# Five of the third group's value tiles ahead of a block stage, three behind it, and all eight heads' queries as blocks

## The chip, the cores and the metric

The kernel runs on one core of one Trainium2 chip. The metric is device time in microseconds (us) of one execution: the median of 3 runs is 1455.4 us (1455.23 to 1455.44). A core has a matrix engine (PE), three others for elementwise work (VectorE or DVE, ScalarE or ACT, GpSimd or POOL), and SyncE (SP), which here only issues transfers. Each engine runs its own instructions strictly in the order in which the program lists them.

## The reference

One encoder layer in fp32 on 1024 tokens of width 1024. All branches read one input projection of the normalised input:

```
h = rms_norm(x) * norm_w
z = h @ w_in        # columns: attention q,k,v of 3 groups x 8 heads x 64, g_a (512),
                    # q_b, zf_fwd, zf_bwd, i_b, g_b (1024 each), zgate_a, zgate_b (1024 each)
# (A) for group g with (window, dilation) in (128,1), (512,4), (2048,16):
s = rms_norm(q) . rms_norm(k) / 8 + bias;  p = exp(s - max);  o_g = p v / sum(p)
o_a = the groups' o_g merged per head, weighted by denominators and maxima
y_a = (o_a * silu(g_a)) @ w_proj_a
# (B) per head of 128: f = lb + (1 - lb) * sigmoid(zf);  S_t = diag(f_t) S_(t-1) + (1 - f_t) i_t^T
o_b = rms_norm(q_b . S forward + q_b . S backward) * silu(g_b);  y_b = o_b @ w_proj_b
x + (sigmoid(zgate_a) * y_a + sigmoid(zgate_b) * y_b) @ w_out
```

Products keep fp32 accuracy: each operand is split into a high part in the matrix engine's fp32r format and the remainder (low part), and high x high, high x low and low x high are summed, three matmuls for each.

## The kernel before

All tiles are 128 partitions by 512 columns unless said otherwise. A weight page of that shape is loaded (`raw`, or `qraw` for blocks), copied by ACT to its high part `whi`, and the low part `wlo` is formed by POOL or DVE. Nine pairs `whi`/`wlo` can be held (RING).

Stages, in the order of PE:
- Values. `tok_group` makes one tile of 128 tokens by 512 value columns: 8 pages by 3 matmuls = 24, called a unit here (PE rows `gp`). A group of values is 8 units, which all read the same 8 pages; the pages come free as the last unit or pair of units goes through them. The first and second groups of heads come first, then the third (`for g in (1, 2)`), in the order of tokens 4, 5, 6, 7, 0, 1, 2, 3. Meanwhile DVE and ACT form the sums `S0` to `S3` of quarters of the input.
- Block stage (`start_quads`, `run_quads`). A block is a product of two 2 x 2 block matrices in 7 products instead of 8 ("11", T1, T2, "21", T3, "22", T4), each 4 x 3 = 12 matmuls into banks `qA`, `qE`, `qC`. Four raw pages make a block's weights (a quad); differences for the T products are formed in place in `qraw` by DVE. The ring of raw pages (QRAW long) gives slots out in order. 27 blocks: 12 for queries and keys (with norms over `nss`), 6 for output gates, 3 for queries `q_b` of heads 0 to 5 (QB), 4 and 2 for the gates.
- i and b columns of the values of branch B (`evac_early`): 16 units in two groups of 8 (`ib_pages`), then 4 units (`T_group`) for the queries of heads 6 and 7. During these `attention_start` opens the attention tiles and queues their loads: the saved quarter `h10D`, keys `ak`, queries `aq`, `abias`, values `av`. The small matmuls of attention (scores `sc`, transposes `pT`, outputs `o`) are put between the units' matmuls by `burst`. DVE adds bias and takes the maximum (`as`, `mst`), ACT takes exponentials.
- Merge of the groups, then branch B head by head, then the output projections.

What sets the order: a planner (`Plan`, `Builder`) runs while the program is written. It keeps a clock for each engine, and at each `tick` puts out the waiting tasks whose inputs it expects to be ready; `b.until` lets its PE clock run on until a condition holds. The instructions then stand in that order for good. `b.BACK` says how far an engine's planned clock may be ahead of PE's for a task still to be put on it.

All engine calls pass through one helper, so every row of the profile names line 58.

Of the kernel before, what the change touches and what calls it, by code (L numbers as in the profile page):

```python
# [26 lines left out]
LEAD = 4  # L27
TAIL, LATE = 4, 4
EARLY = 8
QB = 6  # L30
QRAW, SPARE = 6, 7
LOWS = ("T2", "T4")
SQ, EA = 2, 6
VR, PT = 10, 8
# [2 lines left out]
def _dram(ap, offset, dims):  # L37
    return bass.AP(tensor=ap.tensor, offset=ap.offset + offset, ap=dims)
# [491 lines left out]
class Ring:  # L530
# [30 lines left out]
    def soon(self, n=1):  # L561
        return self.room(n) and self.when(n) <= self.b.p.t["pe"] + self.b.AHEAD
# [60 lines left out]
def hybrid_block(ctx, tc, a, out):  # L623
    b = Builder(ctx, tc, a)
    a_, v_, g_, t_, s_ = b.p.act, b.p.dve, b.p.pool, b.p.pe, b.p.sp
# [7 lines left out]
    last = {}  # L633

    def psum(n):
        order = lambda which: sorted(which, key=lambda i: b.p.free(last[i][0]) if i in last else 0.0)
        b.gps = Banks(b, psp, last, order(range(n)))
        b.bank = Banks(b, psp, last, order(range(n, 8)))
# [11 lines left out]
    stage = b.ring(stg, "stage", 3, [128, 512])  # L650

    def store(dst, t):

        def f():
            s_.dma_start(dst, t)
            stage.done(t)
        b.task("sp", [t], f, 1)
# [4 lines left out]
    some = lambda p, n: [wi[p + k] for k in range(n)]  # L662
# [7 lines left out]
    for k in range(6):  # L670
        blocks += qk[2 * k:2 * k + 2] + sg[k:k + 1] + ([("qb", 2 * k - 2)] if 0 < k <= QB // 2 else [])
    blocks += [("gb", k) for k in range(4)] + [("ga", 0), ("ga", 2)]

    def block_pages(kind, *at):
        if kind == "sg":
            return (*gate_pages(*at), *gate_pages(at[0], at[1] + 1))
        if kind == "ga":
            return tuple(some(72 + 2 * at[0], 4))
        if kind == "qb":
            return (*q_pages(at[0]), *q_pages(at[0] + 1))  # L680
        if kind == "gb":
            return tuple(_dram(wi, (100 + 20 * at[0] + 4 * k) * 65536 + 256 + 128 * col, [[512, 128], [65536, 4], [1, 128]])
                         for col in range(2) for k in range(2))
        g, hv, e = at
        p = 24 * g + 8 + 8 * hv
        return tuple(_dram(wi, (p + 4 * k) * 65536 + 128 * (2 * e + col), [[512, 128], [65536, 4], [1, 128]])
                     for col in range(2) for k in range(2))

    items = some(0, 8) + some(24, 8) + some(48, 8)
    items += [block_pages(*x) for x in blocks]  # L690
    for k in range(2):
        items += ib_pages(k)
    for h in range(QB, EARLY):
        items += q_pages(h)
# [34 lines left out]
    def hs(e, d, t0, n):  # L729

        return hq[e][t0 // 512, d // 4][:, d % 4, t0 % 512:t0 % 512 + n]
# [123 lines left out]
    vD = dr.tile([3, S, 512], F32, name="vD")  # L855
# [28 lines left out]
    def tok_group(p0, t0, evac, last=False, first=None):  # L884
        def step(d):
            wh, wl = b.w[p0 + d]
            vh, vl = first(d) if first else (hs(0, d, t0, 128), hs(1, d, t0, 128))
            return [(vh, wh), (vh, wl), (vl, wh)]

        gr = dict(k=8, step=step, evac=evac, need=lambda d: p0 + d + 1)  # L890
        if last:
            gr["free"] = lambda d: p0 + d + 1
        return gr
# [18 lines left out]
    pos = 0  # L912

    put = {}

    def evac_v(g, t0, scale=None, ring=None):
        def f(ps):
            t = stage.get()  # L920
            a_.activation(t, ps, AF.Copy, **({"scale": scale()} if scale else {}))
            (ring or b.gps).done(ps)
            put[g] = put.get(g, 0) + 1
            if t0 < 0:
                def both():
                    s_.dma_start(vD[g, S - 64:S], t[0:64])
                    s_.dma_start(vD[g, 0:64], t[64:128])
                    stage.done(t)
                b.task("sp", [t], both, 1)
            else:  # L930
                store(vD[g, t0:t0 + 128], t)
        return f

    for d in range(LEAD):
# [96 lines left out]
    def u_group(k, j, t0):  # L1031
        c = slice(128 * j, 128 * j + 128)
        return tok_group(pos, 0, evac_v(1, t0, scale=lambda: rs[k][:, j:j + 1], ring=None if k == 0 else b.bank), first=lambda d: [x[:, c] for x in u_of(k, d)])

    grs = [dict(u_group(1, 3, -64), ring=b.bank)] + [u_group(0, j, A0 + 128 * j) for j in range(4)]
# [70 lines left out]

    for g in (1, 2):
        if g == 2:
            grs = [tok_group(pos, 128 * i, evac_v(g, 128 * i), last=(k >= 6))
                   for k, i in enumerate((4, 5, 6, 7, 0, 1, 2, 3))]  # L1110
        for k, gr in enumerate(grs[:6]):
            if g == 1 and k < 5:
                continue
            b.run_unit([gr])
            if g == 2 and k >= 3:
                blocks_start()
        b.run_unit(grs[6:])
        pos += 8
    b.until(lambda: blocks_start() or "p" in blk)

# [78 lines left out]
         for op, tk in {"11": (0, 0), "21": (0, 1), "T4": (1, 1)}.items()}  # L1199
    for op, k in {"T1": 0, "T2": 1, "T3": 2, "22": 3}.items():  # L1200
        A[op] = [[x[:, c] for c in range(4)] for x in blk["S"][k]]
    b.BACK = 1.2
    b.run_quads(A, [{"qk": put_qk, "sg": put_sg, "ga": put_ga, "gb": put_gb, "qb": put_qb}[x[0]](*x[1:]) for x in blocks],
                [blk["spare"] if x[0] == "qk" else stage for x in blocks])
    b.BACK = 2.5
# [3 lines left out]
    att = {}  # L1209

    def attention_start(now=False):
        if att or not (now or (not b.small and b.quiet())):
            return
        b.drain()
        gctx.close()
        sctx.close()
        p = hctx.enter_context(tc.tile_pool(name="h10b", bufs=1, side="right"))
        psum(2)
        b.eager, b.SLACK = True, 0.25
        ap = actx.enter_context(tc.tile_pool(name="attn", bufs=1))  # L1220
        for n, k, shape in (("v", VR, [128, 256]), ("q", 2, [128, 2, S]), ("k", 2, [128, 2, S]),
                            ("s", 5, [128, 4, 256]), ("pt", PT, [128, 2, 2, 128]), ("os", 2, [128, 2, 2, 128]),
                            ("bias", 2, [128, 4, 256])):
            att[n] = b.ring(ap, "a" + n, k, shape)
        for e in range(2):
            hq[e][1, 0] = p.tile([128, 4, 512], F32R, name=f"hb{'hl'[e]}")
        for c in range(4):
            b.task("sp", [], lambda c=c: back_load(c), 1, stage.soon)
        for o, g in enumerate((1, 2, 0)):
            for hv in range(2):  # L1230
                soon = lambda n, k=2 * o + hv: att[n].soon() and (k == 0 or b.wire(3.5))
                for n, f in (("k", load_k), ("q", load_q), ("bias", load_bias)):
                    b.task("sp", [], lambda g=g, hv=hv, f=f: f(g, hv), 2, lambda n=n, soon=soon: soon(n))
                for i in ((7, 0, 1, 2, 3, 4, 5, 6) if g == 0 else range(8)):
                    b.task("sp", [], lambda g=g, hv=hv, i=i: load_v(g, hv, i), 2, lambda soon=soon: soon("v"))

    def back_load(c):
        t = stage.get()
# [22 lines left out]
    def load_v(g, hv, i):  # L1261
        t = att["v"].get()
        c = slice(256 * hv, 256 * hv + 256)
        if g == 0 and i == 0:
            s_.dma_start(t[0:64], vD[g, 0:64, c])
            s_.dma_start(t[64:128], vD[g, S - 64:S, c])
        elif g == 0:
            s_.dma_start(t, vD[g, 128 * i - 64:128 * i + 64, c])
        else:
            R = (4, 8)[g - 1]  # L1270
            r, half = divmod(i, 8 // R)
            s_.dma_start(t, vD[g].rearrange("(u r) c -> r u c", r=R)[r, 128 * half:128 * half + 128, c])
        V[g, hv, i] = t
# [294 lines left out]
    def evac_early(pr, i):  # L1568
        def f(ps):
            t = stage.get()  # L1570
            a_.activation(t, ps, AF.Copy)
            b.gps.done(ps)
            store(ibD[pr, i], t)
        return f

    def evac_qe(h, u):
# [4 lines left out]
            store(qD[h, u], t)  # L1581
        return f

    for pr in range(2):
        grs = [tok_group(pos, 128 * i, evac_early(pr, i), last=(i >= 6)) for i in range(8)]
        for k in range(7):
            if pr == 0 and k == 4:
                attention_start(True)
                b.until(lambda: att.get("h", 0) == 4)
            b.run_unit(grs[k:k + 1] if k < 6 else grs[6:])  # L1590
            attention_start()
            merge_maybe()
        pos += 8
    for h in range(QB, EARLY):
        for u in range(2):
# [642 lines left out]
    for half in range(2):  # L2238
        for j in range(8):
            def step(d, half=half, n=pos + j):  # L2240
# [4 lines left out]
            gr = dict(k=4, step=step, evac=evac_ya(j, half), need=lambda d, n=pos + j: n + 1,  # L2245
                      ready=lambda half=half: all((d, half) in OA for d in range(4)))
# [179 lines left out]
```

## Time and profile before

| | |
|---|---|
| median of 3 runs | 1455.4 us |
| the profiled execution, span | 1454.89 us, 1453.1 us |
| PE busy | 1444.3 us, 99% |
| DVE, ACT, POOL busy | 968.1, 894.9, 340.3 us |
| third group's value units, last matmul | 142.4 us |
| block stage on PE | 142.65 to 680.7 us |
| first scores of attention | 697.27 us |

Busy time on PE is a sum of overlapping matmuls; the distance from one start to the next is what a matmul adds to the time. In rows of the timeline the columns are start, duration, engine and line, operation, output<-inputs, shapes, count, and in brackets the engine's idle time before it with what ended it.

### The profile page before, as it was taken

Reading aid. Unit: us, or ns where it says so; the run is one execution under the profiler, and the core shown is the slowest. Engines: PE = TensorE matmul, PEld = TensorE weight load, DVE = VectorE, ACT = ScalarE, POOL = GpSimd, SP = SyncE. Lnnn points to the kernel's source line nnn. Section 1 sums busy time; section 2 is a strip of 40 time slices with the busy share of each in tenths; the row PEclk is TensorE's granted clock in tenths of the full one; section 3 lists DMA queues with packets and bytes.
Section 4 is the critical chain, followed back from the end, with each engine's and each line's share of the span. In section 5 each row is a group of like instructions: output and inputs, shape, how many; then the busy total and the mean of one; then the engine's idle time right before and its main releaser. Section 6 shows DMA issues by size and latency. Waiting matters only on the chain.

```text
span 1453.1 us, 22946 instructions
## 1 busy us (share of the span) xinstructions
PE 1444.3 (99%) x7930; PEld 1197.2 (82%) x7930; DVE 968.1 (67%) x1901; ACT 894.9 (62%) x1900; POOL 340.3 (23%) x356
## 2 busy tenths in 40 slices
PE   9999999999999999999999999999999999999998
PEld 8788888888888888888888778888888888788887
DVE  6673678678685788331564649487878786358973
ACT  7743767466565676443688852497777784558461
POOL 0102434464523433333002000031222221001011
PEclk9999999999999999999999999999999999999999
DMA  7746567777643334324848449354444453778665
GB/s 238 181 143 196 165 195 162 192 153 170 148 123 102 98 105 114 111 102 144 280 144 282 151 118 326 123 141 105 126 109 125 110 138 75 225 240 220 181 154 136
DMA packets 194992, 230.75 MB, mean 159 GB/s; under 512 B 46083, under 2 KB 118043, under 8 KB 194364
## 3 DMA queue, kind: packets, MB, share of 16 engines
q1 hardware_dynamic: 180188, 203.93, 45.0%
q0 software_dynamic: 13824, 25.17, 11.7%
q8 instruction: 62, 1.02, 0.3%
q14 instruction: 54, 0.44, 0.1%
q10 hardware_dynamic: 864, 0.19, 0.1%
HBM read 169.29 MB, written 81.43 MB: 173 GB/s over the span
## 4 chain that ended last, share of the span: by engine, by line
PE 90%; DVE 5%; ACT 3%; DMA 1%; issue 1%; SPq 0%; POOL 0%; ACTq 0%; DVEq 0%
PE gp L58 25%; PE qA L58 20%; PE qE L58 10%; PE sA L58 6%; PE qC L58 5%; PE sE L58 5%; PE u L58 3%; PE o L58 3%; PE oB L58 3%; PE pT L58 2%; PE sc L58 2%; PE nss L58 2%; DVE Bc L58 1%; PE U L58 1%; DVE S L58 1%
## 5 line engine op out<-in xcount | busy, mean ns | idle before, releaser
L58 POOL TENSOR_TENSOR wlo<-qraw,whi 128x512 fp32r<-128x512 f32 x135 | 194.3, 1444 | 381.8 <-ACT whi L58 293.8
L58 ACT ACTIVATE whi<-qraw 128x512 fp32r<-128x512 f32 x189 | 117.7, 626 | 100.8 <-DVE qraw L58 43.1
L58 DVE TENSOR_TENSOR qraw<-qraw,qraw 128x512 f32<-128x512 f32 x108 | 100.0, 927 | 39.0 <-POOL wlo L58 28.0
L58 PE MATMUL gp<-hh,whi 128*128 128x512 f32 x264 | 109.7, 416 | 0.0
L58 PE MATMUL gp<-hh,wlo 128*128 128x512 f32 x264 | 103.6, 393 | 0.0
L58 PE MATMUL gp<-hl,whi 128*128 128x512 f32 x264 | 103.0, 390 | 0.0
L58 ACT ACTIVATE as<-as,neg 128x192 f32<-128x192 f32 (+2 forms) x192 | 83.8, 442 | 16.8 <-DVE neg L58 16.7
L58 ACT ACTIVATE whi<-raw 128x512 fp32r<-128x512 f32 x92 | 57.6, 627 | 43.8 <-PE gp L58 18.7
L58 PE MATMUL qA<-hh,whi 128*128 128x512 f32 x216 | 84.4, 391 | 0.0
L58 PE MATMUL qA<-hh,wlo 128*128 128x512 f32 x216 | 84.3, 390 | 0.0
L58 DVE CUSTOM_DVE_ANT_0 as<-sc,abias 128x192 f32<-128x192 f32 (+2 forms) x192 | 56.0, 348 | 42.4 <-PE sc L58 27.1
L58 PE MATMUL qA<-hl,whi 128*128 128x512 f32 x216 | 84.0, 389 | 0.0
L58 POOL COPY mm<-Bc 128x8 f32<-128x8 f32 x64 | 32.2, 534 | 205.6 <-DVE Bc L58 123.6
L58 PE MATMUL gp<-whi,hh 128*128 128x512 f32 x192 | 78.6, 409 | 0.0
L58 PE MATMUL gp<-wlo,hh 128*128 128x512 f32 x192 | 75.2, 391 | 0.4 <-DVE wlo L58 0.4
L58 PE MATMUL gp<-whi,hl 128*128 128x512 f32 x192 | 75.0, 391 | 0.0
L58 DVE TENSOR_TENSOR wlo<-qraw,whi 128x512 fp32r<-128x512 f32 x54 | 37.3, 691 | 49.6 <-ACT whi L58 49.6
L58 DVE SCALAR_TENSOR_TENSOR ny<-ny,spare 128x512 f32<-128x512 f32 x48 | 67.4, 1405 | 1.6
L58 ACT ACTIVATE ny<-ny 128x512 f32<-128x512 f32 x96 | 60.8, 633 | 4.0 <-DVE ny L58 0.8
L58 PEld LDWEIGHTS gp<-hh,wlo 128*128 128x128 f32 x264 | 49.5, 188 | 11.0
L58 POOL DMA_DIRECT2D wlo<-in_w_in_dram x36 | 31.5, 875 | 113.6 <-ACT wlo L58 97.8
L58 PEld LDWEIGHTS gp<-hh,whi 128*128 128x128 f32 x264 | 49.8, 188 | 8.3
(306 smaller groups left out, 4208.2 us busy)
## 6 DMA issues: line engine op xcount, KB each, us to landing
qraw<-in_w_in_dram SPq DMA_DIRECT2D x108, 256.0 KB, 3.8
raw<-in_w_in_dram SPq DMA_DIRECT2D x84, 256.0 KB, 3.7
qkD<-ny SPq DMA_DIRECT2D x48, 256.0 KB, 2.8
wlo<-in_w_in_dram POOLq DMA_DIRECT2D x36, 256.0 KB, 4.4
sg<-sgD SPq DMA_DIRECT2D x32, 256.0 KB, 3.7
eraw<-wsD SPq DMA_DIRECT2D x32, 256.0 KB, 3.3
sgD<-stage SPq DMA_DIRECT2D x26, 256.0 KB, 2.7
ak<-qkD SPq DMA_DIRECT2D x6, 1024.0 KB, 6.6
```

Of the source, the lines that this page charges most:

```text
L58: got = f(*args, **kw)
```

## The change

The third group's value pages are loaded twice. Five of its units (tokens 4, 5, 6, 7, 0) stand ahead of the block stage, three (1, 2, 3) behind it. The queries of heads 6 and 7 become one more block (28 in all) and their four units go. Attention is opened as soon as the block stage is over, ahead of the three value units, and the 16 i and b units all follow; the last group of 8 ends in single units. Loads of the third group's values wait until all eight of its tiles are stored (`wrote`). QRAW goes from 6 to 5, SPARE (tiles that hold block results) from 7 to 8, and BACK stays at 2.5 in the block stage, where it was 1.2.

```diff
-QB = 6
-QRAW, SPARE = 6, 7
+QB = 8
+NV = 5
+QRAW, SPARE = 5, 8
...
     items += [block_pages(*x) for x in blocks]
+    items += some(48, 8)
...
-                store(vD[g, t0:t0 + 128], t)
+                def keep():
+                    s_.dma_start(vD[g, t0:t0 + 128], t)
+                    stage.done(t)
+                    wrote[g] = wrote.get(g, 0) + 1
+                b.task("sp", [t], keep, 1)
...
         if g == 2:
-            grs = [tok_group(pos, 128 * i, evac_v(g, 128 * i), last=(k >= 6))
-                   for k, i in enumerate((4, 5, 6, 7, 0, 1, 2, 3))]
-        for k, gr in enumerate(grs[:6]):
-            if g == 1 and k < 5:
-                continue
+            grs = [tok_group(pos, 128 * i, evac_v(g, 128 * i), last=(i == NV - 5)) for i in (4, 5, 6, 7, 0, 1, 2, 3)[:NV]]
+        for gr in grs[5 * (2 - g):-2]:
             b.run_unit([gr])
-            if g == 2 and k >= 3:
+        for gr in (grs[-2:-1], grs[-1:]) if g == 2 else (grs[-2:],):
+            b.run_unit(gr)
+            if g == 2:
                 blocks_start()
-        b.run_unit(grs[6:])
         pos += 8
...
-    b.BACK = 1.2
...
-                    b.task("sp", [], lambda g=g, hv=hv, i=i: load_v(g, hv, i), 2, lambda soon=soon: soon("v"))
+                    b.task("sp", [], lambda g=g, hv=hv, i=i: load_v(g, hv, i), 2,
+                           lambda g=g, soon=soon: (g < 2 or wrote[g] == 8) and soon("v"))
...
+    attention_start(True)
+    grs = [tok_group(pos, 128 * i, evac_v(2, 128 * i), last=(i > 1)) for i in range(NV - 4, 4)]
+    for k in range(3 - NV + 4):
+        b.run_unit(grs[k:k + 1] if k < 2 - NV + 4 else grs[-2:])
+    pos += 8
+    b.until(lambda: att.get("h", 0) == 4)
     for pr in range(2):
-        grs = [tok_group(pos, 128 * i, evac_early(pr, i), last=(i >= 6)) for i in range(8)]
-        for k in range(7):
-            if pr == 0 and k == 4:
-                attention_start(True)
-                b.until(lambda: att.get("h", 0) == 4)
-            b.run_unit(grs[k:k + 1] if k < 6 else grs[6:])
+        n = 6 + pr
+        grs = [tok_group(pos, 128 * i, evac_early(pr, i), last=(i >= n)) for i in range(8)]
+        for k in range(n + 1):
+            b.run_unit(grs[k:k + 1] if k < n else grs[n:])
             attention_start()
             merge_maybe()
```

How the instructions move is shown at two places. First, ACT where the block stage begins: `stage` rows are evacuations of value units, `whi_` rows splits of the first quad (1255, 1257, 1259, 1261 are its raw pages, 1263 the next quad's first), `spare` rows evacuations of its first products. Before:

```order
L58 ACT_TABLE_LOAD
L58 ACTIVATE whi_1279<-qraw_1255 128x512
L58 ACTIVATE stage_1290<-gp_1248 128x512
L58 ACTIVATE stage_1320<-gp_1293 128x512
L58 ACTIVATE whi_1331<-qraw_1255 128x512
L58 ACTIVATE whi_1349<-qraw_1255 128x512
L58 ACTIVATE whi_1353<-qraw_1261 128x512
L58 ACTIVATE whi_1371<-qraw_1257 128x512
L58 ACTIVATE whi_1375<-qraw_1263 128x512
L58 ACTIVATE whi_1387<-qraw_1259 128x512
L58 ACTIVATE stage_1405<-gp_1323 128x512
```

And the same place on ACT in the changed kernel:

```order
L59 ACT_TABLE_LOAD
L59 ACTIVATE whi_1277<-qraw_1255 128x512
L59 ACTIVATE stage_1288<-gp_1248 128x512
L59 ACTIVATE whi_1295<-qraw_1255 128x512
L59 ACTIVATE spare_1311<-qA_1291 128x512
L59 ACTIVATE whi_1317<-qraw_1255 128x512
L59 ACTIVATE whi_1321<-qraw_1261 128x512
L59 ACTIVATE spare_1336<-qE_1313 128x512
L59 ACTIVATE whi_1341<-qraw_1257 128x512
L59 ACTIVATE whi_1345<-qraw_1263 128x512
L59 ACTIVATE whi_1349<-qraw_1259 128x512
```

Before, six splits stand ahead of the last value units' evacuations and so ahead of the first product; now the second split stands behind the last value unit, and the third behind the evacuation of the first product.

Second, ACT where attention begins: `hbh` is the saved quarter's high part, `as` rows with `neg` are exponentials, `apt` copies of transposes. Before, from the first unit behind the block stage:

```order
L58 ACTIVATE stage_6184<-gp_6157 128x512
L58 ACTIVATE hbh<-stage_6201 128x512
L58 ACTIVATE hbh<-stage_6203 128x512
L58 ACTIVATE stage_6256<-gp_6197 128x512
L58 ACT_TABLE_LOAD
L58 ACTIVATE as_6284,mst_104<-as_6284,neg_6288 128x192 x4
L58 ACTIVATE hbh<-stage_6236 128x512
L58 ACTIVATE stage_6346<-gp_6258 128x512
L58 ACTIVATE hbh<-stage_6251 128x512
L58 ACTIVATE as_6285,mst_104<-as_6285,neg_6288 128x192 x4
L58 ACTIVATE apt_6379<-pT_6369 128x512
```

In the changed kernel, from the evacuation of the second and third value unit on (these two units run as a pair):

```order
L59 ACTIVATE stage_6386<-gp_6290 128x512
L59 ACTIVATE whi_6389<-raw_6263 128x512
L59 ACT_TABLE_LOAD
L59 ACTIVATE as_6353,mst_104<-as_6353,neg_6357 128x192 x4
L59 ACTIVATE hbh<-stage_6281 128x512
L59 ACTIVATE stage_6430<-gp_6291 128x512
L59 ACTIVATE whi_6442<-raw_6313 128x512
L59 ACTIVATE whi_6449<-raw_6325 128x512
L59 ACTIVATE whi_6453<-raw_6333 128x512
L59 ACTIVATE apt_6467<-pT_6457 128x512
L59 ACTIVATE as_6354,mst_104<-as_6354,neg_6357 128x192 x4
```

Splits of i and b pages now stand among the first exponentials, the first of them (raw_6263) directly ahead of them; before, there were none.

More of the change, by code (lines that the diff above doesn't have):

```diff
@@ L912, in hybrid_block @@
     pos = 0
-    put = {}
+    put, wrote = {}, {}
     def evac_v(g, t0, scale=None, ring=None):
```

## The prediction

> **What bounds the kernel now.** I read the page's totals and its chain first, then TensorE's (PE's) own waits, then the timelines at the two places where the change shortens a cover: the start and the end of the block stage.
>
> ```profile
> span 1453.1 us, 22946 instructions
> PE 1444.3 (99%) x7930; PEld 1197.2 (82%) x7930; DVE 968.1 (67%) x1901; ACT 894.9 (62%) x1900; POOL 340.3 (23%) x356
> PEclk9999999999999999999999999999999999999999
> PE 90%; DVE 5%; ACT 3%; DMA 1%; issue 1%; SPq 0%; POOL 0%; ACTq 0%; DVEq 0%
> ...
> PE warm L58 <- DVE warm L58: 1.4, 1, 1.4
> PE alT L58 <- issue: 0.8, 1, 0.8
> PE sc L58 <- DVE mst L58: 0.4, 1, 0.4
> PE pT L58 <- ACT apt L58: 0.2, 1, 0.2
> ```
>
> PE is busy in 99% of the span at full granted clock, and its named waits are of 1.4 us and less. So the time is the number of matmuls times their spacing. A matmul taken away gains its spacing, a new wait on PE is paid in full, and work on other engines costs only where PE comes to wait for it.
>
> The spacing is read from the timeline, start to start (start, duration, what):
>
> ```profile
> 654.63 0.39 PE L58 MATMUL qA<-S2h,wlo 128*128 128x512 f32 x1
> ...
> 676.39 0.39 PE L58 MATMUL qE<-S3h,wlo 128*128 128x512 f32 x1
> ```
>
> These are the first and the last of 97 rows: 21.76 us / 96 = 0.2267 us each. The duration of 0.39 us overlaps the next matmul and is no price.
>
> **The sum, part by part.**
>
> *The queries of heads 6 and 7.* Out go 4 units of 24 matmuls, in comes one quad of 7 products of 12: 96 - 84 = 12 matmuls fewer, 12 x 0.2267 = -2.72 us. [...] The copies that come with quad and units (28 units become 24) run off PE.
>
> *The three value tiles moved.* Their 72 matmuls are the same, so 0 on PE. They need the group's 8 weight pages a second time, while 4 query pages leave the same stretch: net 4 loads, 4 whi on ACT and 4 wlo on POOL more beside attention. What that hides under is the attention start, below.
>
> *PE's interleaving beside attention.* A stretch of small matmuls between projections costs something at its borders:
>
> ```profile
> 721.57 1.03 PE L58 MATMUL pT<-ident,as 128*128 128x128 f32 x8
> 722.36 0.47 PE L58 MATMUL gp<-whi,hh 128*128 128x512 f32 x1
> 722.68 0.39 PE L58 MATMUL gp<-wlo,hh 128*128 128x512 f32 x1
> 722.90 0.40 PE L58 MATMUL gp<-whi,hl 128*128 128x512 f32 x1
> 723.23 1.57 PE L58 MATMUL sc<-ak,aq 64*128 64x192 f32 x16
> 724.73 0.50 PE L58 MATMUL gp<-whi,hh 128*128 128x512 f32 x1
> 725.07 0.40 PE L58 MATMUL gp<-wlo,hh 128*128 128x512 f32 x1
> ```
>
> Before scores a projection takes 0.33 us instead of 0.23 (722.90 to 723.23), after them 0.34 (724.73 to 725.07): +0.2 us a stretch; a stretch of transposes pays only at its end (722.36 to 722.68), +0.1 us. In the order of the whole program the stretches go from 145 to 148, the changes of kind inside them (transposes, outputs, scores) from 36 to 33. At +0.1 to +0.3 us for the one and up to -0.1 for the other this is 0 to +0.9 us; I take +0.4, since the added borders are with scores and outputs.
>
> *The start of the block stage.* After the fourth value unit the quads are started; then four units remain as cover before the first product, in the changed kernel one.
>
> ```profile
> 122.20 3.26 SPq L58 DMA_DIRECT2D qraw<-in_w_in_dram  x6
> 125.37 0.63 ACT L58 ACTIVATE whi<-qraw 128x512 fp32r<-128x512 f32 x1 [2.33 <-issue]
> 126.08 1.29 POOL L58 TENSOR_TENSOR wlo<-qraw,whi 128x512 fp32r<-128x512 f32 x1 [68.11 <-DMA qraw<-in_w_in_dram]
> 126.33 0.39 PE L58 MATMUL gp<-whi,hh 128*128 128x512 f32 x1
> 127.41 0.69 DVE L58 TENSOR_TENSOR qraw<-qraw,qraw 128x512 f32<-128x512 f32 x1 [8.81 <-POOL wlo L58]
> 142.65 0.39 PE L58 MATMUL qA<-hh,whi 128*128 128x512 f32 x1
> ...
> L58 POOL TENSOR_TENSOR wlo<-qraw,whi x135: 1283/1298/2507, 126.1 to 654.2; 128x512 fp32r<-128x512 f32 x135
> L58 DVE TENSOR_TENSOR qraw<-qraw,qraw x108: 658/687/2470, 127.4 to 654.3; 128x512 f32<-128x512 f32 x108
> DMA to landing us min/median/max: 2.5/3.8/8.7
> ```
>
> Now PE begins the products at 142.65; in the changed order the fifth unit ends at 126.33 and the products follow at once. Everything up to 122.20 stands in the same order, so these rows hold. The first product's two leading matmuls need whi (there at 126.0); the third needs wlo, done at 127.37: it would start at 126.78 and starts at 127.4, a stall of 0.6 us. The second (T1) goes through DVE 127.41 to 128.1, whi to 128.8, wlo to 130.1, wanted at 130.15: 0.1. The third (T2: 0.69 on DVE, 0.63 whi, 0.69 low part on DVE) is ready at 132.4, wanted at 132.9. From there the pages gain on PE: each costs POOL 1.3 us at most and a product takes PE 2.72.
>
> QRAW=5 brings a second tie. The ring gives slots out in order, so four loads of the next quad wait for this quad's last split (T4, DVE behind the evacuation of "21": about 139.4). Issued at 139.6, landed at the median 3.8 later at 143.4, then 0.69 + 0.63 + 1.3 and 0.4 for the handovers: ready at 146.4. It is the ninth product, whose low part PE wants at about 150: 3.6 us of slack, so it holds up to a landing of 7.4 us. The next one (T2) stands on DVE behind a norm's Newton steps and has about 1.5 us. From the third quad on T4's split stands eight products ahead on DVE, which gives over 9 us to land.
> Sum here +0.8 us; ends 0 (the low part in time) and +7 (the late-landing rival).
>
> *The attention start.* Now the i and b units cover it; the drain and the loads come one unit after the last product (680.69), since that is when the queue is quiet.
>
> ```profile
> 680.69 0.39 PE L58 MATMUL gp<-whi,hh 128*128 128x512 f32 x1
> 681.51 0.34 SPq L58 DMA_DIRECT2D gaD<-spare  x1
> 688.48 0.37 SPq L58 DMA_DIRECT2D ak<-qkD  x1
> 689.40 0.47 SPq L58 DMA_DIRECT2D abias<-skewD  x1
> 689.91 9.09 SPq L58 DMA_DIRECT2D av<-vD  x8
> 697.27 2.22 PE L58 MATMUL sc<-ak,aq 64*128 64x192 f32 x24
> 698.93 0.36 DVE L58 CUSTOM_DVE_ANT_0 as<-sc,abias 128x192 f32<-128x192 f32 x1 [6.75 <-DMA av<-vD]
> 699.04 0.91 SPq L58 DMA_DIRECT2D stage<-h10D  x2
> 699.91 0.43 PE L58 MATMUL sc<-ak,aq 64*128 64x192 f32 x1 [0.41 <-DVE mst L58]
> 700.37 0.45 ACT L58 ACTIVATE as<-as,neg 128x192 f32<-128x192 f32 x1 [6.21 <-DVE neg L58]
> 703.95 0.63 ACT L58 ACTIVATE hbh<-stage 128x512 fp32r<-128x512 f32 x1 [1.72 <-DMA stage<-h10D]
> 692.00:696.00 4.00, 4.00 (x19) 3.31 (x18) 0.18 (x1) 1.88 (x2) 0.00 (x0) 1.00 1.01 402
> 704.00:708.00 4.00, 4.00 (x32) 3.35 (x31) 2.37 (x7) 3.20 (x10) 0.31 (x1) 1.00 1.03 408
> ```
>
> The scores meet a bias that has only just landed (DVE at 698.93), which costs PE about 0.7 us now (its wait of 0.41 at 699.91, and the scores' slower pace ahead of it). In the changed kernel the loads are queued right after the last store (681.51), some 4 us earlier, and that wait goes: -0.7. In its place weight pages stand in ACT's line ahead of the first exponentials: the first i and b page that is not yet loaded is issued behind the eight av loads. Those took SP 9.1 us with the DMA engines full (share 1.01), so counted from the store at 681.5 it is issued about 695, and at the 4.9 us from issue to use that h10D shows (699.04, the issue behind the av loads, to 703.95) it lands about 700. ACT then has its whi (0.63), a table load (1.3) and four exponentials (1.8): done at 703.5, where PE, after 66 + 6 + 12 projections and two stretches of scores, wants the transposes at 703.1. Three more pages follow on ACT (1.6 us) and one by one on POOL (3.9 us), and PE wants them 0.23 x 3 = 0.7 us apart after 705: about 1 us late in sum. Taken: +0.4 + 1.0 - 0.7 = +0.7, beside -0.2 for the transposes' wait that this order no longer has: +0.5. Ends -0.9 (old waits gone, no new one) and +4.
>
> *The rest.* The third group's value loads now wait until all eight tiles are stored; they stand behind the second group's sixteen, so 0. BACK and SPARE act through the order alone, which is priced above. The order after attention keeps its rows; nothing is put down for it.
>
> Sum: -2.72 + 0.4 + 0.8 + 0.5 = -1.0 us. The profiled execution took 1454.9 us (its span and 1.8 around it), 0.5 under the median of 1455.4: 1453.9 on its own terms, **1454.4 us** against the median. A change under 0.2% (2.9 us) counts as none; a measurement of this kernel tells little less from nothing.
>
> **The rivals.**
>
> *Faster: no new stall.* If the low parts are in time at the block start and the old waits at the attention start go, -2.72 + 0.4 - 0.9 = -3.2, or 1452.2 us. For it: PE waits nowhere else in the block stage. Against it: 127.37 for the first low part is a row, not a guess.
>
> *Slower: the split chain never gets ahead.* The place is the first ten quads, where ACT's order puts splits only 4 to 6 products ahead of PE (9 to 11 before). The price is the landing: at the maximum of 8.7 us the ninth product is 1.3 us late, and a quad's cycle becomes 8.7 to land, 2.6 for T1 (0.69 + 0.63 + 1.3), 2.0 for T2 and 5.2 for four pages on POOL, 18.5 us with nothing between (13.6 at the median), against 19.0 of PE. Each hold by evacuations then shows, some 0.7 us a quad over ten quads: +7 and 1461 us. It decides from a landing of about 7.4 us; the median of 3.8 speaks against it. Where a difference meets a low part on POOL it has taken up to 2.47 us, though the median is 0.69, so part of the holds are real. [...] The median row of 687 ns says that here most do not meet.
>
> *Slower: pages late beside attention.* If the added loads, at 4 x 256 KB over 300 GB/s 3.5 us of full DMA, land ahead of nothing, exponentials and pages wait 4 us and more: about 1458.5 us. For it: a DMA share of 1.01 to 1.03 through 708. Against it: the loads start 4 us earlier.
>
> **How the numbers follow.** The forecast (within 2.9 us of no change) has 0.60; the late landing 0.18; late pages 0.10, both counted as slower; no new stall 0.12. The range of 8 in 10 reaches down to the third case, 1452.3, and up into the slower ones without the end of the first, 1460. The forecast's own range is 1452.6 to 1457.5, from the bounds of borders (0 to 0.9) and starts.
>
> **What would show it.** After: 12 matmuls fewer at 0.2267 us; qA's first row near 126.3 and its third near 127.4; no PE wait at a wlo after the third product; scores without the 0.7 us wait; ACT's first exponential near 702. Wrong would be: PE waits of over 1 us in 130 to 330, a landing row of qraw above 7 us, gaps before pT or gp in the 30 us after the last product.

## The result and the profile after

The changed kernel takes 1469.55 us (median of 4 runs, 1466.73 to 1471.19) against 1455.42 us: a ratio of 1.0095, 95% interval 1.0082 to 1.0108. It is slower by 14 us, where 1 us less was forecast and 1460 was the upper end of the range. The profiled execution of it, 1466.73 us, is the shortest of the four; the others had granted clocks of 0.996 to 0.998 in place of its 0.999, to which a finding below returns.

The page of the changed kernel, its totals and its chain (all calls are on line 59 now, since one line was added above the helper):

```profile
span 1465.0 us, 22942 instructions
PE 1446.2 (99%) x7918; PEld 1195.0 (82%) x7918; DVE 969.5 (66%) x1906; ACT 898.3 (61%) x1911; POOL 361.3 (25%) x369
PEclk9999999999999999999999999999999999999999
PE 74%; DVE 9%; issue 7%; ACT 5%; POOL 3%; DMA 3%; SPq 1%; POOLq 0%; DVEq 0%; ACTq 0%
```

The 12 matmuls are gone (7930 to 7918) and PE's busy time has hardly moved, but the chain that ends last runs through PE for 74% where it was 90%. The totals cannot tell more; PE's waits (total, times, longest) and the stretches (PE, weight loads, DVE, ACT, POOL busy, granted clock, DMA share, GB/s) tell where:

```profile
PE nss L59 <- DVE ny L59: 4.8, 2, 2.9
PE gp L59 <- ACT stage L59: 2.8, 2, 2.0
PE qA L59 <- DVE stage L59: 2.6, 2, 1.4
...
PE nss L59 <- DVE nlo L59: 1.0, 1, 1.0
...
PE qA L59 <- POOL wlo L59: 0.5, 1, 0.5
```

```profile
350.00:400.00 50.00, 49.37 (x217) 40.77 (x218) 31.55 (x42) 30.70 (x53) 26.54 (x22) 1.00 0.62 138
400.00:450.00 50.00, 45.59 (x199) 36.71 (x198) 30.91 (x38) 24.86 (x43) 21.33 (x18) 1.00 0.67 168
450.00:500.00 50.00, 47.14 (x200) 38.27 (x199) 38.46 (x47) 33.99 (x60) 19.33 (x14) 0.97 0.29 79
```

Before, each such stretch of the block stage held 220 to 222 matmuls. Here 400 to 450 us and 450 to 500 us hold 199 and 200: some 9 us are lost in the middle of the block stage, some 270 us behind the place that the prediction looked at most. PE waits there for sums of norms (`nss`) and for banks that an evacuation has to free (`qA <- stage`), and only once, for 0.5 us, for a weight.

The first and the last matmul of the block stage, from the rows of `qA` before and after (count; shortest, median, longest ns; first and last start):

```profile
L58 PE MATMUL qA<-hh,whi x216: 389/389/398, 142.7 to 680.0; 128*128 128x512 f32 x108
L58 PE MATMUL qA<-hh,wlo x216: 388/389/397, 143.1 to 680.5; 128*128 128x512 f32 x108
```

```profile
L59 PE MATMUL qA<-hh,whi x224: 387/389/628, 126.7 to 695.9; 128*128 128x512 f32 x112
L59 PE MATMUL qA<-hh,wlo x224: 388/389/628, 127.9 to 696.3; 128*128 128x512 f32 x112
```

The stage took 537.8 us and takes 569.6. Its 84 matmuls more are 19.0 us of that; the other **12.8 us** are lost. Ahead of it 72 matmuls (16.3 us) went. Behind it PE needs 765.0 us instead of 769.0, of which 24 fewer matmuls are 5.4, so 1.5 us are lost there. Together -16.3 + 31.8 - 4.0 and 0.4 by which the front of this execution ran later: 11.9 us, the difference of the two spans. So the question is the 12.8 us.

What happens at such a place is seen on DVE (start, duration; idle time before it and what ended it) and on SP, from 398 to 421 us of the changed kernel:

```profile
398.45 0.69 DVE L59 TENSOR_TENSOR wlo<-qraw,whi 128x512 fp32r<-128x512 f32 x1 [0.34 <-ACT whi L59]
399.06 1.28 DVE L59 TENSOR_TENSOR nlo<-ny,nhi 128x512 fp32r<-128x512 f32 x2
404.80 0.69 DVE L59 TENSOR_TENSOR qraw<-qraw,qraw 128x512 f32<-128x512 f32 x1 [4.45 <-issue]
407.56 0.69 DVE L59 TENSOR_TENSOR qraw<-qraw,qraw 128x512 f32<-128x512 f32 x1 [2.07 <-POOL wlo L59]
...
408.77 0.68 DVE L59 TENSOR_TENSOR nlo<-ny,nhi 128x512 fp32r<-128x512 f32 x1
410.98 0.69 DVE L59 TENSOR_TENSOR wlo<-qraw,whi 128x512 fp32r<-128x512 f32 x1 [1.53 <-ACT whi L59]
...
412.19 1.20 DVE L59 TENSOR_TENSOR qraw<-qraw,qraw 128x512 f32<-128x512 f32 x1
413.31 0.68 DVE L59 TENSOR_TENSOR nlo<-ny,nhi 128x512 fp32r<-128x512 f32 x1
413.91 0.68 DVE L59 SCALAR_TENSOR_TENSOR ny<-nss,ny 128x512 f32<-128x512 f32 x1
414.51 1.45 DVE L59 SCALAR_TENSOR_TENSOR spare<-spare,nqk,ny 128x512 f32<-128x512 f32 x1
416.00 2.07 DVE L59 SCALAR_TENSOR_TENSOR ny<-ny,spare 128x512 f32<-128x512 f32 x1
417.99 1.79 DVE L59 TENSOR_TENSOR qraw<-qraw,qraw 128x512 f32<-128x512 f32 x1
```

```profile
398.79 2.64 SPq L59 DMA_DIRECT2D qraw<-in_w_in_dram  x4
```

The last low part of a quad (398.45) frees the raw slots; the next quad's four loads go out at once (398.79), and DVE stands at the first difference for 4.45 us; the profile names no releaser there, but the loads are what that difference reads. Then it stands 2.07 us for POOL. The norms queued behind come late: PE waits at 409.5 for the `nlo` of 408.77. Then DVE stands 1.53 us for a split (410.98) and a difference takes 1.20 us (412.19), so the `ny` that empties the bank of `nss` ends at 414.59, and PE waits for it until 414.7. Behind that three steps in a row take 1.45, 2.07 and 1.79 us. The weights themselves were in time: reading each product's start against the end of its low part, they were 5 to 20 us ahead in every quad from the eleventh to the eighteenth, where PE waited most. So it is DVE's other work, behind the splits in the same line, that PE waits for.

### The profile page after: what moved, and what is told of

The parts are those of the page before. It is cut to its first block, busy times and chain, and to the rows that moved or that the text cites. A ratio compares the mean times of both kernels' runs of the same rounds, so it can differ in the third digit from the quotient of the medians.

```text
span 1465.0 us, 22942 instructions
## 1 busy us (share of the span) xinstructions
PE 1446.2 (99%) x7918; PEld 1195.0 (82%) x7918; DVE 969.5 (66%) x1906; ACT 898.3 (61%) x1911; POOL 361.3 (25%) x369
## 4 chain that ended last, share of the span: by engine, by line
PE 74%; DVE 9%; issue 7%; ACT 5%; POOL 3%; DMA 3%; SPq 1%; POOLq 0%; DVEq 0%; ACTq 0%
PE gp L59 25%; PE qA L59 12%; PE sA L59 6%; PE qE L59 6%; PE sE L59 5%; PE u L59 3%; PE o L59 3%; PE oB L59 3%; POOL wlo L59 3%; PE qC L59 3%; PE sc L59 2%; PE pT L59 2%; DMA qraw<-in_w_in_dram 1%; DVE qraw L59 1%; ACT ny L59 1%
## 5 line engine op out<-in xcount | busy, mean ns | idle before, releaser
L59 POOL TENSOR_TENSOR wlo<-qraw,whi 128x512 fp32r<-128x512 f32 x140 | 202.1, 1456 | 386.5 <-ACT whi L59 308.9
L59 DVE TENSOR_TENSOR qraw<-qraw,qraw 128x512 f32<-128x512 f32 x112 | 108.0, 967 | 87.9 <-POOL wlo L59 60.0
L59 PE MATMUL gp<-hh,whi 128*128 128x512 f32 x240 | 100.3, 418 | 0.0
L59 PE MATMUL gp<-hh,wlo 128*128 128x512 f32 x240 | 94.3, 393 | 0.0
L59 PE MATMUL gp<-hl,whi 128*128 128x512 f32 x240 | 93.7, 391 | 0.0
L59 PE MATMUL qA<-hh,whi 128*128 128x512 f32 x224 | 88.5, 395 | 2.6 <-DVE stage L59 2.6
L59 PE MATMUL qA<-hh,wlo 128*128 128x512 f32 x224 | 88.2, 394 | 0.5 <-POOL wlo L59 0.5
L59 DVE TENSOR_TENSOR wlo<-qraw,whi 128x512 fp32r<-128x512 f32 x56 | 41.9, 749 | 43.6 <-ACT whi L59 39.4
L59 ACT ACTIVATE ny<-ny 128x512 f32<-128x512 f32 x96 | 60.8, 633 | 16.3 <-DMA qkD<-ny 9.1
L59 POOL TENSOR_TENSOR wlo<-raw,whi 128x512 fp32r<-128x512 f32 x25 | 32.0, 1284 | 131.4 <-ACT whi L59 131.2
L59 ACT ACTIVATE spare<-qA 128x512 f32<-128x512 f32 x52 | 30.7, 591 | 44.1 <-PE qA L59 44.1
```

Of the source, the lines that this page charges most:

```text
L59: got = f(*args, **kw)
```

## The experiments

"Lost in the block stage" below is the time from the first to the last matmul of the stage, less its matmuls (`nss` among them) times 0.2267 us, less the 2.2 us that the kernel before shows by this reading. "Lost behind it" is the time from there to the last matmul of the kernel against 768.95 us, less 0.2267 us for each matmul fewer (more for more). Both come from one profiled execution and hold the matmuls that ran at half clock behind a wait (last section): 1.2 to 2.6 us in the stage of those kernels that had any. Executions of one kernel differ by up to 5 us, so a column and a median can disagree: the profiled execution of ring6_back12 was 4 us above its median. The last column was not taken apart for every kernel. The times are medians, the ratios are to the kernel before in the same series.

| kernel | us | ratio, 95% | lost in block stage | lost behind |
|---|---|---|---|---|
| changed | 1469.6 | 1.0095 (1.0082-1.0108) | 12.8 | 1.5 |
| ring6 | 1466.6 | 1.0077 (1.0062-1.0092) | 10.9 | 3.4 |
| back12 | 1463.6 | 1.0057 (1.0040-1.0074) | 8.6 | 3.4 |
| ring6_back12 | 1460.9 | 1.0043 (1.0026-1.0059) | 6.6 | 6.2 |
| before_ring5_back25 | 1468.2 | 1.0088 (1.0073-1.0103) | 11.2 | 1.2 |
| only_qb8 | 1462.5 | 1.0057 (1.0044-1.0070) | 0.0 | 9.9 |
| only_ring5 | 1459.9 | 1.0038 (1.0024-1.0052) | 4.4 | 0.1 |
| only_back25 | 1467.0 | 1.0082 (1.0068-1.0096) | 11.4 | -1.6 |
| only_tiles | 1462.8 | 1.0055 (1.0043-1.0068) | 6.7 | 0.4 |
| priced | 1461.8 | 1.0048 (1.0034-1.0062) | 6.4 | 4.4 |
| before_back06 | 1460.7 | 1.0035 (1.0022-1.0049) | 3.7 | 2.6 |
| before_back17 | 1467.6 | 1.0079 (1.0062-1.0095) | 11.2 | 3.6 |
| qb8_late5 | 1462.9 | 1.0054 (1.0041-1.0066) | 0.0 | 11.2 |
| nv6 | 1465.2 | 1.0078 (1.0063-1.0093) | 7.7 | 4.9 |
| numbers_undone_priced | 1461.9 | 1.0058 (1.0041-1.0074) | 6.6 | 1.6 |
| before_priced | 1460.6 | 1.0041 (1.0026-1.0056) | 6.0 | 0.1 |
| before_cover2 | 1458.5 | 1.0021 (1.0011-1.0031) | 4.2 | -0.7 |
| nv6_cover2 | 1460.6 | 1.0033 (1.0020-1.0047) | 4.0 | 5.0 |

### The three numbers: ring, spare tiles, BACK

The first theory was the ring: five raw slots, as in the rows above. Its rivals were the short cover at the start of the stage, and BACK.

```diff
-QRAW, SPARE = 5, 8
+QRAW, SPARE = 6, 7     # ring6, ring6_back12
...
+    b.BACK = 1.2           # back12, ring6_back12, ahead of run_quads
```

> The changed kernel with QRAW and SPARE back at 6 and 7 and nothing else undone. Three theories of the 12 us that PE lost in waits inside the block stage. Ring: with five slots the first loads of a quad are issued only behind the last split of the quad before, so VectorE stands at the first difference until they land, and the norms and evacuations queued behind it are late; then this kernel loses at most 2 us in the block stage and takes 1455 to 1458 us. Cover: the quads begin with one value unit as cover instead of four, and the splits, which start level with PE, never gain a lead; then a sixth slot is worth little and it takes 1465 us or more. BACK: the order of ACT and VectorE is planned too far ahead; then nothing changes and it takes 1466 to 1471 us.

> The changed kernel with BACK at 1.2 in the block stage again, QRAW and SPARE left at 5 and 8. Ring: VectorE still waits for the first loads of each quad, 1465 us or more. Cover: the same, 1465 us or more. BACK: the block stage loses 2 us at most, 1455 to 1458 us.

> The changed kernel with both undone: QRAW and SPARE at 6 and 7, BACK at 1.2. Ring and BACK theories: 1454 to 1457 us, since what is left of the change was priced at -1.0 us on 1455.4 and lost 1.5 more at the attention start. Cover: 1463 us or more, with PE still waiting on VectorE in the quads between 350 and 500 us.

`before_ring5_back25` is the kernel before with the opposite edits (5, 8 and 2.5).

> The kernel before with only the three numbers of the change: QRAW and SPARE at 5 and 8, BACK at 2.5, with four value units of cover, six heads' queries as blocks and no value tile moved. Ring or BACK: 1463 us or more, with PE waits on VectorE in the block stage. Cover: 1455 to 1457 us, since the lead of some 15 us at the first product is kept.

The ring theory fell as it was put: six slots give 3 us back, not 12. BACK alone gives 6 and both together 8.7, so BACK weighs most and 5.5 us are neither. back12 and ring6_back12 came out between the branches written down for them, so no single theory held. The kernel before with nothing but the three numbers loses 11.2 us in its block stage, with its cover of four units untouched.

Then each part of the change alone, on the kernel before:

```diff
-QB = 6
+QB = 8                  # only_qb8
...
-QRAW, SPARE = 6, 7
+QRAW, SPARE = 5, 8      # only_ring5
...
-    b.BACK = 1.2
+    b.BACK = 2.5           # only_back25
```

> The kernel before with QRAW and SPARE at 5 and 8 alone; BACK stays at 1.2. In the changed kernel undoing this alone gave 3 us and undoing BACK alone 6 us. If the ring's price does not depend on BACK: 1457 to 1460 us, with VectorE's idle time before differences well over the 39 us of before. If a lead of 15 us at the first product hides it: 1455 to 1456 us.

> The kernel before with BACK at 2.5 in the block stage alone; the ring stays at 6. If planning ACT and VectorE further ahead costs by itself: 1459 to 1464 us, with PE waiting on evacuations and norms in many quads while the splits keep their lead of 17 to 22 us. If it costs only together with five slots: 1455 to 1457 us.

The two separate cleanly on DVE. Its idle time before differences between 130 and 690 us (total, times, longest), in the kernel before, in only_ring5 and in only_back25:

```profile
DVE qraw L58 <- POOL wlo L58: 19.2, 9, 7.3
DVE qraw L58 <- DMA qraw<-in_w_in_dram: 11.0, 4, 5.0
```

```profile
DVE qraw L58 <- POOL wlo L58: 61.5, 25, 7.1
DVE qraw L58 <- DMA qraw<-in_w_in_dram: 19.9, 8, 5.3
DVE qraw L58 <- issue: 3.0, 3, 1.9
```

```profile
DVE qraw L58 <- DMA qraw<-in_w_in_dram: 18.6, 8, 4.1
DVE qraw L58 <- POOL wlo L58: 15.9, 7, 7.2
```

Five slots make DVE stand 84 us instead of 30 at its differences (79 in the changed kernel), and that costs PE 4.4 us: most of it is idle time of an engine that has a third of its time free. BACK at 2.5 makes DVE stand hardly longer than before, 34 us, and costs 11.4; its time is 3 us above the range given for a cost of BACK by itself. So standing is not what costs most. PE's waits in only_back25, and DVE ahead of the one at 419 us:

```profile
PE nss L58 <- DVE ny L58: 6.8, 4, 1.8
```

```profile
409.26 0.69 DVE L58 TENSOR_TENSOR wlo<-qraw,whi 128x512 fp32r<-128x512 f32 x1 [0.44 <-ACT whi L58]
409.87 0.69 DVE L58 TENSOR_TENSOR qraw<-qraw,qraw 128x512 f32<-128x512 f32 x1
410.47 0.68 DVE L58 TENSOR_TENSOR spare<-qE,spare 128x512 f32<-128x512 f32 x1
411.07 0.68 DVE L58 SCALAR_TENSOR_TENSOR ny<-nss,ny 128x512 f32<-128x512 f32 x1
411.67 1.54 DVE L58 SCALAR_TENSOR_TENSOR spare<-spare,nqk,ny 128x512 f32<-128x512 f32 x1
413.24 1.09 DVE L58 SCALAR_TENSOR_TENSOR ny<-ny,spare 128x512 f32<-128x512 f32 x1
...
416.85 1.78 DVE L58 TENSOR_TENSOR qraw<-qraw,qraw 128x512 f32<-128x512 f32 x1
418.55 0.69 DVE L58 SCALAR_TENSOR_TENSOR ny<-nss,ny 128x512 f32<-128x512 f32 x1
```

Twelve instructions, the last of them the one that frees the bank, fill DVE from 409.26 to 419.24 with hardly a gap. The planner counts 0.61 us for each (`pace = max(0.19, 0.076 + n / 960.0)`), 7.3 us for twelve beside the meetings with POOL that it foresees; they took 10.0. Of the 2.7 us too much, 2.0 are two meetings with POOL's low parts (the rows of 1.54 and 1.78, beside low parts that POOL began at 411.36 and 416.69) and 0.4 the norm's step of 1.09; how much of the meetings the planner foresaw is not shown. PE's own order was fixed by that clock, and PE stands at `nss`.

### The planner's price of a norm's step, and BACK at other values

The last step of a norm reorders its columns for the second and third group of heads. In the kernel before it takes 0.69 us in the first group, 1.08 in the second and 1.18 in the third (medians of the rows with no low part on POOL beside them), and 1.67 to 2.44 us in 20 of its 48 rows, all of them beside a low part. `priced` tells the planner so:

```diff
                 elif op == "tensor_tensor_scan":
                     pace = 1.25
+                elif op == "scalar_tensor_tensor" and len(out.ap) > 2:
+                    pace = 1.1
```

> The changed kernel, whose planner is told what the trace shows for one operation: VectorE's last step of a norm with reordered columns (groups 1 and 2) takes 1.07 to 1.2 us alone, where the planner counts 0.61. All numbers of the change stay (five raw slots, BACK 2.5). PE's waits of the changed kernel begin at 350 us, where the norms of group 1 are under way. If VectorE runs late because the planner's clock of it is too fast: the waits between 340 and 500 us go and it takes 1457 to 1461 us. If it is the place in the line (evacuations and norms behind splits) whatever the price: 1465 us or more.

The block stage loses 6.4 us instead of 12.8: the waits between 340 and 500 us are gone but for 0.3 to 0.5 us, as was expected if the planner's clock was the reason, and one of 2.2 us is left near 565. The time is 0.8 us above the range given for this, with 4.4 us lost behind the stage, most of it at the first value unit's evacuation (a wait of 3.0 us) and at half clock behind it (granted clock 0.997 over this execution). So half of the loss goes with the price of this step. The same edit on two other kernels:

> ring6_back12 with the planner told 1.1 us for a norm's reordering step. Its waits in the block stage lie before 230 us, in the norms of group 0, whose step takes 0.69 us; the order there does not change. So the price can give nothing there: 1459 to 1462 us. Under 1458 us would say that the price acts in another way than through the norms of groups 1 and 2.

> The kernel before with the planner told 1.1 us for the same step. Before loses 2.2 us in its block stage over the bare sum of its matmuls, so the right price has little to win: 1454 to 1456 us if the order stays as good, 1458 us or more if any new order of ACT and VectorE costs, as with BACK at 0.6 and 1.7.

With the numbers undone the price gives nothing in the stage, as expected (6.6 and 6.6 us), since the waits left there lie in the first group. In the kernel before it is a loss of 6 us: one new wait of 3.0 us on an evacuation near 600 us, and 2.6 us at half clock behind it (granted clock 0.998 over this execution; the last section has such a place). A truer price is no cure by itself; any new order is a new throw, and so the 6.4 us in the changed kernel are not shown to be the price alone. The same is seen in BACK:

> The kernel before with BACK at 0.6 in the block stage, nothing else. If the price of BACK is steady, less planned ahead is no worse: 1453 to 1456 us. If 1.2 is only the point at which this order happens to fit, 0.6 costs too: 1458 us or more.

> The kernel before with BACK at 1.7 in the block stage, between 1.2 and 2.5. If the cost grows with BACK: 1458 to 1463 us, between 1455 and the 1467 us of 2.5. If the order merely fits or does not: anything from 1455 to 1468 us, unrelated to the size of the step.

0.6, 1.2, 1.7 and 2.5 lose 3.7, 0, 11.2 and 11.4 us in the stage. Less planned ahead is not better either; the order at 1.2 happens to have no wait. That the loss jumps between 1.2 and 1.7 and then stays is measured, not explained.

### The moved tiles and the cover

`only_tiles` is the changed kernel with QB, QRAW, SPARE and BACK as before.

> The changed kernel with QB back at 6, QRAW and SPARE at 6 and 7 and BACK at 1.2: of the change only the three value tiles behind the block stage are left, and the order of attention's start that goes with them. ring6_back12 took 1460.9 us; if the seven products' gain of 2.7 us is in it, this takes 1463 to 1464 us, and PE's waits are those of a short cover: one at the first wlo (0.6 us) and some 4 us at the norms of the first four quads, before the splits have a lead. If the cover is not the cause of those waits, 1456 to 1458 us.

```profile
PE nss L59 <- ACT ny L59: 2.7, 1, 2.7
...
PE qA L59 <- ACT spare L59: 1.1, 1, 1.1
...
PE qA L59 <- POOL wlo L59: 0.5, 1, 0.5
```

6.7 us are lost in the block stage, all before 230 us: 0.7 at the first low part, 2.8 at a norm near 195 us, 1.4 at half clock behind that wait (granted clock 0.999 over this execution), 1.3 at an evacuation near 225. Behind the block stage it loses 0.4. To see whether the short cover does it, the quads' start was moved alone:

```diff
-            if g == 2 and k >= 3:
+            if g == 2 and k >= 5:     # before_cover2
```

```diff
-NV = 5
+NV = 6                   # nv6, nv6_cover2
...
             b.run_unit([gr])
+            if g == 2 and gr is grs[3]:
+                blocks_start()     # nv6_cover2
```

`nv6` is ring6_back12 with six value tiles ahead of the stage. It was meant to have two units of cover, and its expectation says so wrongly: its quads start one unit later as well, so the cover stays at one. `nv6_cover2` starts them after the fourth unit, which makes it two.

> ring6_back12 (the changed kernel with QRAW and SPARE at 6 and 7, BACK at 1.2; 1460.9 us, 6.6 us of it lost in the block stage) with six value tiles ahead of the block stage and two behind it (NV = 6), so two units of cover instead of one. If the short cover makes the early waits: the block stage loses 1 to 3 us and it takes 1455 to 1458 us. If they come from how the order of norms happens to fall: 1460 us or more.

> The kernel before, whose quads start after the sixth value unit of the third group instead of the fourth: two units of cover instead of four, all else as before. If the short cover is what the moved tiles cost in the block stage: the first product meets weights some 5 us ahead instead of 15.7, and the stage loses 3 to 7 us, 1458 to 1462 us. If the lead at the start is of no matter: 1454 to 1457 us.

> nv6 (1465.2 us, 7.7 us lost in its block stage beyond what the kernel before loses there) with the quads started after the fourth value unit, so that two units follow before the first product instead of one. If the short cover makes the loss: the wait of 0.65 us at the first wlo goes, and the stage loses 2 to 5 us, 1459 to 1463 us. If not, the loss stays within 1 us.

One unit of cover loses 6.6, 6.7 and 7.7 us (ring6_back12, only_tiles, nv6), of which 1.2 to 1.4 are at half clock; two lose 4.2 and 4.0 in two otherwise different kernels, with no half clock (granted clock 1.000 in both profiled executions); four lose 0. Between the two-unit kernels even the waits agree: 1.9 us near 210 and 199 us, 1.0 and 0.9, then 0.6. So the loss follows the cover, though again not where the prediction had it: with two units every low part is at least 3 us early, and PE still waits, for norms. That the splits, while they catch up, go ahead of the norms on ACT and DVE is the likely reason; it was not tested.

### The queries of heads 6 and 7

> The kernel before with one part of the change: all eight heads' queries as blocks (QB = 8, 28 quads), and the four value units for heads 6 and 7 gone. If the price of 12 matmuls at 0.2267 us (-2.72 us) holds and nothing else comes with it: 1452 to 1453.5 us, the fastest of all so far. If the 28th quad itself upsets the order of the norms, or the cover beside attention was needed, 1455 us or more.

In the block stage the 28th quad costs nothing beyond its matmuls. The loss, 9.9 us, is where the four units were, and its largest piece is this wait at the first transposes of branch B:

```profile
PE kT L58 <- DVE sk L58: 4.9, 1, 4.9
```

```profile
940.68 0.69 DVE L58 TENSOR_TENSOR macc<-macc,gal 128x512 f32<-128x512 f32 x1
...
944.51 1.22 DVE L58 TENSOR_TENSOR_SCAN Bc<-rst,qr 128x512 f32<-128x512 bf16 x1 [2.54 <-ACT qr L58]
```

DVE is at the merge until 941 us, branch B's loads wait for that, and PE has run out of units. `qb8_late5` puts two gate units of the end there:

```diff
-TAIL, LATE = 4, 4
+TAIL, LATE = 4, 5
```

> The kernel before with all heads' queries as blocks (QB = 8) and two of the last gate units put ahead of branch B's first projections (LATE = 5), where only_qb8 lost 5 us: there PE waited at the first transpose of branch B for VectorE, which was busy with the merge until 941 us since the four query units that had covered it were gone. Two units are 48 x 0.2267 = 10.9 us of cover. If that wait was the missing cover: 1452 to 1456 us. If the merge and the loads behind it simply move along, or the end misses the two units: 1460 us or more.

```profile
PE gp L58 <- ACT xh L58: 5.7, 1, 5.7
```

The wait at `kT` is gone, and one of 5.7 us stands near 1248 us, where the two units had been. The cover was moved, not won. None of the kernels beats the one before.

## Why the prediction was wrong, by its own steps

**12 matmuls, -2.72 us.** They went, and nothing speaks against the spacing: every stretch without a wait holds 220 to 223 matmuls in 50 us. "Run off PE" was too light: only_qb8 shows that the four units were the cover of the merge. In the changed kernel, which has the three moved tiles behind the block stage, that wait is absent.

**The start of the block stage, +0.8 us.** What was worked out held. The low part of the first product stalls PE by 0.7 us (0.6 forecast), the second is on time with 0.15 us to spare, the ninth has 4.0 us of slack (3.6 forecast), the one behind it 1.7 (1.5 forecast). (Two sums are off by 0.1: the stalls worked out, 0.6 and 0.1, give 0.7 and not 0.8, and the case without a new stall is 1452.2 in one place and 1452.3 in the other. Neither matters here.)

**"From the third quad on T4's split stands eight products ahead on DVE, which gives over 9 us to land", and "BACK and SPARE act through the order alone, which is priced above".** This is the step that failed: the block stage was put at +0.8 us and lost 12.8. The order was priced only by whether a weight is there when PE wants it. Weights never held PE again after the third product, as forecast, and the rest went all the same, in the norms and evacuations that stand in the same lines. BACK, put at nothing beyond that, loses 11.4 us in the stage alone (only_back25), and with the ring and SPARE 11.2 (before_ring5_back25).

**The rival "the split chain never gets ahead in the first ten quads", 1461 us, 0.18.** It had the side, the ring and the holds of evacuations behind differences. Its place was wrong (the largest waits lie in quads 12 to 18), its condition too (it asked for landings above 7.4 us; they took 4.0 us in the median and 6.5 at most), and its price was half of what came. Its sentence on differences that meet a low part on POOL, read from the rows, deserved more weight. In the changed kernel a step that takes 1.08 us alone took 2.07 (416.00), and a difference, 0.69 us in the median, took 1.79 (417.99), while POOL was at low parts:

```profile
414.13 5.10 POOL L59 TENSOR_TENSOR wlo<-qraw,whi 128x512 fp32r<-128x512 f32 x3 [0.54 <-ACT whi L59]
```

Of the 112 differences of the changed kernel 35 began while a low part was running; 33 of these ended 0.55 us after that low part did, the other two took 0.68 and 0.74 us. No difference that began otherwise took over 1 us.

**Beside attention, +0.4 and +0.5 us.** 1.5 us were lost behind the block stage, near enough in sum, but not by the mechanism named. The scores no longer wait for a bias, as said. The first value unit's evacuation stands on ACT behind the split of the reloaded quarter:

```profile
702.10 1.29 ACT L59 ACTIVATE hbh<-stage 128x512 fp32r<-128x512 f32 x2 [4.23 <-DMA stage<-h10D]
704.21 0.60 ACT L59 ACTIVATE stage<-gp 128x512 f32<-128x512 f32 x1 [0.81 <-DVE hbl L59]
```

PE waits 2.0 us for it at 704.86. The late pages that were feared there did not come.

**The forms of the effect.** The ring with SPARE, BACK and the tiles lose 4.4, 11.4 and 6.7 us alone in the stage and 12.8 together, not 22.5. That a line which is already late hides a second delay would explain it, and was not tested. Why a given order has no wait and its neighbour has five stays open; what is shown is which parts cost how much, that half of the loss goes with the price of one DVE step in the changed kernel, and that the tiles' part follows the cover.

## What to carry to other kernels

When a change reorders engines that are planned in advance, price every consumer in the reordered lines, not only the operand that the main engine asks for next: list what frees PE's banks and where that stands. A number that only sets how far ahead a planner works is not free; here it cost 11.4 us, four times what the 12 matmuls taken away were worth. And work taken from the main engine may have been the cover of something: ask what it hid before counting it as a gain.

## What the runs showed of the hardware

A wait of PE can cost more than its length. Behind the longest wait of the changed kernel:

```profile
491.01 0.39 PE L59 MATMUL qA<-S2h,wlo 128*128 128x512 f32 x1
494.26 0.50 PE L59 MATMUL nss<-nhi,headones 128*128 128x512 f32 x1 [2.86 <-DVE ny L59]
...
495.62 0.63 PE L59 MATMUL qA<-hh,whi 128*128 128x512 f32 x1
...
498.61 0.49 PE L59 MATMUL qA<-hl,whi 128*128 128x512 f32 x1
```

From 1.1 us after the end of the wait the spacing is 0.43 us in place of 0.23 for seven matmuls, 1.4 us in all; the granted clock is 0.50 from 495.38 to 498.79, and 0.97 over 450 to 500 us. From start to start the gap is 3.25 us here. The six other gaps of over 1 us in this execution, 1.15 to 2.40 us, have no half clock in them or behind them. In the block stage half clock cost 1.2 to 1.4 us in the kernels with one unit of cover and 2.6 in before_priced.

The length of the longest wait does not decide it alone. The granted clock over the profiled execution is 1.000 in before_ring5_back25 and nv6_cover2, where PE's longest waits are 2.8 and 3.0 us, and 0.999 in only_back25 and the changed kernel, where they are 1.8 and 2.9. What decides it is not shown. The timed runs of the changed kernel that are 2 to 4.5 us longer than the profiled one had granted clocks of 0.996 to 0.998; no profile shows where those lost it.
